# Token tiles 3 and 4 in places that the order sees apart, and A's scores kept negated with a running minimum

## The chip, the cores and the metric

The kernel runs on one core of a Trainium2 chip. A core has a tensor engine (PE in the profile, its weight loads are PEld), a vector engine (DVE), a scalar engine (ACT), a general engine (POOL) and a queue engine (SP) that issues all of this kernel's transfers between the chip's main memory (DRAM) and its on-chip memory. Matrix products land in eight banks of a separate accumulation memory (PSUM). Each engine runs its own instructions strictly in the order in which they were written and waits at an instruction until what it needs has been made by the others. The metric is the device time of one execution in microseconds (us), as the median of several.

## What is computed

One layer of a hybrid encoder over 1024 prompt tokens and 32 sample tokens of width 1024. Cut to what matters here:

```python
hn = rmsnorm(h, g_pre)
qa, ka, va, ga, qb, kb, vb, gb = split(hn @ w_in)           # 8 x 512 columns

# A: band attention, 8 heads of 64
s = einsum('bqhd,bkhd->bhqk', q, k) * ATTN_SCALE
s = s + bias_table[:, clip(k_pos - q_pos, -128, 128) + 128]
s = where(ok, s, -1e30)                                     # own chunk of 64 and 8 before it
oa = softmax(s) @ v

# B: stick-breaking attention, 8 heads of 64 (products of sigmoids along the keys)

y = concat(oa * silu(ga), ob * silu(gb)) @ w_out
h = h + rmsnorm(y, g_post)
h = h + sigmoid(h @ w_ple_gate) * (p @ w_ple)               # "PLE"
```

The keys and values of A and B are outputs too. Everything is float32; a product is made from a high and a low part of each factor (`...h` and `...l`), in three matrix products.

## The kernel before

**The order is made by the program.** The kernel's code does not emit instructions, it records them (`Recorder.add`, line 308). For each argument the recorder keeps a buffer and a *box*: the range of rows and columns that the view covers. An operation comes after every earlier one whose box in the same buffer overlaps its own, if one of the two writes (lines 318 to 330). A view keeps its box exact through slices; `rearrange` (line 76) keeps the box it had and marks all its dimensions unknown, so a slice taken after a `rearrange` still has the box of the whole. `order` (line 372) then plays the engines against modelled costs (`cost`, line 338) and takes for each engine, at each time, the ready operation with the lowest key: its class (`cls` for PE, `low` for the others), then its place in the recording. A transfer that comes after another transfer is ready only when the model has that one landed (lines 417 to 420 and 432). A buffer from a ring (a `tag` with `bufs` places) may be taken when all uses of the buffer that held the place before are done (lines 202 and 374 to 376). What comes out is the written order of each engine; on the chip the waits follow the real addresses.

**The start of the kernel** (lines 1334 to 1400). Nine token tiles of 128 rows (the ninth has the 32 sample tokens) are loaded (`load_x`, line 565), normed and scaled (`scale_x`, line 579: a square with its sum on ACT, two tiny POOL instructions for `rs`, two DVE instructions of 512 columns that multiply by `rs` and by the row `gpre`), transposed on PE four squares at a time (`turn_x`, line 588: a PSUM bank `ptx`, a copy on ACT to `hnh`, a difference on DVE to `hnl`), and so become the right-hand side of the input projection. That is worked off in three chunks of 352 tokens; the first needs tiles 0, 1 and a part of 2, the second goes to the middle of tile 5. For the first column groups kA, qA and vA of the projection (`mm_kA`, `mm_qA`, `mm_vA`) the chunks stand one behind the other. Their weights (`wr_...`) are split into parts by POOL. PE also does a piece of the PLE product for tiles 0 to 3 here (`ple`, six matmuls of 512 columns for each of two halves of a tile, `pieces`, line 1157).

Tiles 0, 1, 2 and 5 to 8 take places in a ring of 3076 columns (`om` in the profile). Tiles 3 and 4 lie in one buffer `x34` (`x` in the profile), in the room that later holds `wTh`.

The PSUM banks: two "mm" for the projection, three "S", two "T" for transposes, one "PV". All `ptx` are from "T". Two of the "S" banks hold the two halves of `gpre` until the last tile is scaled; the third takes the early PLE product of tile 2, first half. Its second half takes the place of the first `gpre`.

**Attention** (`attention`, line 778) runs through eight pairs of heads, A and B in turn, while PE fills up with the projection of the next pair. For a block of 128 queries of A: two matmuls per piece of scores into an "S" bank; on DVE one instruction that adds the bias and takes the maximum along the way (lines 843 to 846; two, the second going on from the first's maximum, where the scores have two pieces; the profile shows it as `CUSTOM_DVE_ANT_0` with a short accumulator read behind it); on DVE the maximum is negated (line 848, `statA<-statA TENSOR_SCALAR`); on ACT the Exp with that as its bias and with its sum; on DVE the reciprocal; on POOL the product; then transposes (`ptwA`) for the values. There are 64 such blocks, and two groups for the sample tokens (`sample_attention`, line 949). The bias comes from a table of eight rows that `bias_rows` (line 606) builds and stores to DRAM; `begin` loads it for a head, and POOL writes -1e30 into two corners. The queries are scaled by 1/8 when ACT takes them from the accumulator (line 748); the sample tokens' queries (`qsS`) are cut from the same place.

```python
dma(xt[0:n], x_prompt[0, t * P:t * P + n, :] if t < 8 else x_sample[0])     # load_x
...
pt = psum(TURN.get((t, kh), "T"), f"ptx{t}_{kh}")                           # turn_x
...
acc = psum(("S", "PV")[t - 2] if t > 1 and self.early else "mm" if self.early else "S", f"ple{t}_{q}")
```

Of the kernel before, what the change touches and what calls it, by code (L numbers as in the profile page):

```python
# [8 lines left out]
F32 = mybir.dt.float32  # L9
F32R = mybir.dt.float32r  # L10
AF = mybir.ActivationFunctionType
ALU = mybir.AluOpType

P = 128
D = 1024
# [7 lines left out]
HD = 64  # L23
NEG = -1e30
EPS = 1e-6
SCALE = HD ** -0.5
# [429 lines left out]
def stream_step(  # L456
# [7 lines left out]
    nc = rec  # L464
# [47 lines left out]
    at = rec.pool(at_stack, tc, name="at", bufs=1)  # L512
    opnd = [at0, at]
    ring0, ring1 = Arena(rec, at, "om", 3076), Arena(rec, at, "be", 3640)
# [48 lines left out]
    x34 = []  # L563

    def load_x(t):
        n = min(P, T - t * P)
        if t == 3:
            x34.append(at.tile([P, ringh.cols], F32, tag="wTh", name="x34")[:, 0:2 * D].rearrange("p (a c) -> p a c", a=2))
        xt = x34[0][:, t - 3] if t in (3, 4) else ring0.tile([P, D], f"x{t}")
        dma(xt[0:n], x_prompt[0, t * P:t * P + n, :] if t < 8 else x_sample[0])  # L570
        return xt, n

    HALF = [slice(0, 512), slice(512, 1024)]
    TURN = {}

    def norm_tile(t, xt, n, gp):
        return turn_x(t, scale_x(t, xt, n, gp), n)
# [28 lines left out]
    def bias_rows():  # L606

        rb = ring0.tile([8, 257], "rb")
        dma(rb, rel_bias[0])
        R = ring1.tile([8, 768], "R")  # L610
        nc.gpsimd.memset(R, 0.0)
        nc.vector.tensor_scalar(R[:, 256:768], R[:, 256:768], rb[:, 0:1], None, ALU.add)
        nc.vector.tensor_copy(R[:, 0:256], rb[:, 0:256][:, ::-1])
        dma(r_dr, R)

# [96 lines left out]
    def col_steps(j):  # L712

        kind, p = order[j]
        ab, k = kind[1], kind[0]
        n = sidx(ab, p)
        box = {}
        steps = []

        def mms(c, part):  # L720
            if part == 0:
                if c == 0:
                    ensure(j)
                    ensure(j + 1)
                    if k != "g":
                        box["st"] = at2.tile([P, T], F32, tag="stg", name=f"st{kind}{p}", bufs=3)
                box["acc"] = psum("mm", f"mm_{kind}{p}_{c}")[:, 0:CH]
            acc = box["acc"]
            cs = slice(c * CH, (c + 1) * CH)
            if k == "g" and part == 0:  # L730
                box["og"] = at2.tile([P, CH], F32, tag="bias", name=f"og{kind}{p}_{c}", bufs=2)
                dma(box["og"], o_dr[n][:, cs])
            W = loaded[j]
            for x in range(part * 24 // PARTS, (part + 1) * 24 // PARTS):
                q, k8 = x // KD, x % KD
                a = W[k8 // 4][1 if q == 1 else 0]
                b = (hnl if q == 2 else hnh)[c]
                nc.tensor.matmul(acc, a[:, k8 % 4, :], b[:, k8, :], start=(x == 0), stop=(x == 23))
            if part < PARTS - 1:
                return  # L740
            if k == "g":
                sg = at2.tile([P, 512], F32, tag="sg", name=f"sg{kind}{p}_{c}", bufs=3)[:, 0:CH]
                nc.scalar.activation(sg, acc, AF.Sigmoid)
                nc.vector.tensor_tensor(sg, acc, sg, ALU.mult)
                nc.gpsimd.tensor_tensor(sg, sg, box["og"], ALU.mult)
                dma(og_dr[n, :, cs], sg)
            elif k == "q":
                nc.scalar.activation(box["st"][:, cs], acc, AF.Copy, scale=SCALE)
            else:
                nc.scalar.copy(box["st"][:, cs], acc)  # L750

        for c in range(NCH):
            for part in range(PARTS):
                steps.append((3.6 / PARTS, lambda c=c, part=part: mms(c, part), GATE_NEEDS.get((kind, p)) if part == 0 else None))

        def after_q():
            src_of["q", ab, p] = box["st"]
            nc.gpsimd.tensor_scalar(qsS[:, slot(ab, p), :], box["st"][:, SEQ:T], 1.0, 1.0, ALU.mult, ALU.mult)

        def after_k():  # L760
            src_of["k", ab, p] = box["st"]
            nc.gpsimd.tensor_scalar(ksS[:, slot(ab, p), :], box["st"][:, SEQ:T], 1.0, 1.0, ALU.mult, ALU.mult)

        def after_v(tok):
            src_of["v", ab, p] = tok
            dma(vs_dr[ab][:, p * P:(p + 1) * P], tok[0:NS, 8, :])

        if k == "q":
            steps.append((0.0, after_q))
        elif k == "k":  # L770
            steps.append((0.0, after_k))
            steps += keys_out(ab, p, lambda: box["st"], *((ak_p, ak_s) if ab == "A" else (bk_p, bk_s)))
        elif k == "v":
            steps += values_out(ab, p, lambda: box["st"], *((av_p, av_s) if ab == "A" else (bv_p, bv_s)), after_v)
        return steps


    def attention(ab, p, h):
# [3 lines left out]
        box = {}  # L782

        def begin():
            if ab == "A":
                bias = at2.tile([P, 640], F32, tag="bias", name=f"bias{nm}", bufs=2)
                dma(bias, bias_src(2 * p + h, P, 0, 640))
                nc.gpsimd.memset(bias[0:HD, 0:HD], NEG)
                nc.gpsimd.memset(bias[HD:P, 576:640], NEG)
                box["bias"] = bias  # L790

        def lo_block(i):
# [20 lines left out]
        def scores(i):  # L813
            L, kd, kl = Lq[h], KDh[h], KLD[h]
            b0 = lo_block(i)
            n = (i + 1 - b0) * P
            k0 = b0 * P
            cut = [0, n] if n <= 512 else [0, n // 2, n]
            w0, w1 = rooms(i)
            pieces = []  # L820
            for j in range(len(cut) - 1):
                s = psum("S", f"S{nm}_{i}_{j}")[:, 0:cut[j + 1] - cut[j]]
                lhs = L[:, i * P:(i + 1) * P]
                ks = slice(k0 + cut[j], k0 + cut[j + 1])
                nc.tensor.matmul(s, lhs, kd[:, ks], start=True, stop=False)
                nc.tensor.matmul(s, lhs, kl[:, ks], start=False, stop=True)
                pieces.append((cut[j], cut[j + 1], s))
            if ab == "B":
                a, b, s = pieces[-1]
                dg = s[:, b - a - P:b - a]  # L830
                nc.vector.tensor_tensor(dg, dg, maskb, ALU.add)
                nc.gpsimd.memset(w0[:, n:n + 1], 1.0)
                for a, b, s in pieces:
                    nc.scalar.activation(w0[:, a:b], s, AF.Sigmoid, scale=-1.0)
                for a, b, s in pieces:
                    nc.scalar.activation(w1[:, a:b], s, AF.Sigmoid)
                for a, b, s in reversed(pieces):
                    rev = w0[:, a + 1:b + 1][:, ::-1]
                    nc.vector.tensor_tensor_scan(rev, rev, s, 1.0 if b == n else w0[:, b + 1:b + 2], ALU.mult, ALU.bypass)
                nc.gpsimd.tensor_tensor(w1[:, 0:n], w1[:, 0:n], w0[:, 1:n + 1], ALU.mult)  # L840
            else:
                m = small.tile([P, 4], F32, tag="stat", name=f"stat{nm}_{i}", bufs=6)
                for j, (a, b, s) in enumerate(pieces):
                    nc.vector.tensor_tensor_reduce(
                        w0[:, a:b], s, box["bias"][:, n - b:n - a][:, ::-1], 1.0,
                        -3e38 if j == 0 else m[:, j - 1:j], ALU.add, ALU.max, m[:, j:j + 1])
                last = len(pieces) - 1
                nc.vector.tensor_scalar(m[:, 2:3], m[:, last:last + 1], -1.0, None, ALU.mult)
                nc.scalar.activation(w1[:, 0:n], w0[:, 0:n], AF.Exp, bias=m[:, 2:3], accum_out=m[:, 3:4])
                nc.vector.reciprocal(m[:, 3:4], m[:, 3:4])  # L850
                nc.gpsimd.tensor_scalar(w1[:, 0:n], w1[:, 0:n], m[:, 3:4], 1.0, ALU.mult, ALU.mult)
            state[i] = w0, w1
# [96 lines left out]
    def sample_attention(ab, gi):  # L949
# [6 lines left out]
        NK = PAST + NS  # L956
# [38 lines left out]
        def scores():  # L995
# [20 lines left out]
            else:  # L1016
                m = small.tile([P, 4], F32, tag="stat", name="stat" + nm, bufs=6)
                for j, (a0, b0, s) in enumerate(pieces):
                    nc.vector.tensor_tensor_reduce(
                        w0[:, a0:b0], s, bx["bias"][:, NK - b0:NK - a0][:, ::-1], 1.0,  # L1020
                        -3e38 if j == 0 else m[:, 0:1], ALU.add, ALU.max, m[:, j:j + 1])
                nc.vector.tensor_scalar(m[:, 2:3], m[:, 1:2], -1.0, None, ALU.mult)
                nc.scalar.activation(w1[:, 0:NK], w0[:, 0:NK], AF.Exp, bias=m[:, 2:3], accum_out=m[:, 3:4])
                nc.vector.reciprocal(m[:, 3:4], m[:, 3:4])
                nc.gpsimd.tensor_scalar(w1[:, 0:NK], w1[:, 0:NK], m[:, 3:4], 1.0, ALU.mult, ALU.mult)
            bx["w1"] = w1
# [829 lines left out]
```

## Time and profile before

| | |
|---|---|
| median of 3 runs | 796.58 us (795.9 to 797.61) |
| the profiled execution | 795.36 us, its span 793.6 us |
| tensor engine clock granted | 1.00 |
| busy: PE, PEld, DVE, ACT, POOL | 778.3, 717.3, 589.7, 537.7, 468.4 us |
| moved by the DMA engines | 153.66 MB, 194 GB/s in the mean |

How to read the rows that follow. In a stretch's row stand its bounds and length, then for PE, PEld, DVE, ACT and POOL the busy time and in brackets the number of instructions, then the granted clock, the busy share of the DMA engines and GB/s. A row of a timeline has the start, the busy time, the engine, the operation, out<-in, the shape and the count of instructions merged into it, and in square brackets how long the engine stood idle before it and what ended that. A row of waits has the engine with the tile it worked on, what it waited for, and the us in total, the times and the longest. A row of a group has the count, then the busy time in us and the mean ns of one, then the idle time before. SPq is the queue engine, and its rows show the issue of a transfer, not its landing; a row of issues gives the KB of each and the median us to landing. Matmuls overlap, so PE's pace is read from the starts, not from the durations.

### The profile page before, as it was taken

To read this page: it belongs to the slowest core of one execution; us is meant where nothing else is said; L and a number is where in the kernel's file an instruction comes from. 1 tells how busy PE (TensorE), PEld (TensorE's weight loads), DVE (VectorE), ACT (ScalarE), POOL (GpSimd) and SP (SyncE) were. 2 spreads that over 40 slices of the span, in tenths; PEclk is the share of its full clock that TensorE was granted. 3 is DMA by queue.
4 is the path that set the end of the run, shared out by engine and by line. 5 is a ranking of instruction groups with operands and counts; after the bars stand their busy time and mean duration, and the time that the engine had idled before them with its cause. 6 is when DMAs were issued, how large, how long until landed. Compare 5 with 4: busy or idle time off the path is not lost.

```text
span 793.6 us, 14512 instructions
## 1 busy us (share of the span) xinstructions
PE 778.3 (98%) x4606; PEld 717.3 (90%) x4606; DVE 589.7 (74%) x1170; ACT 537.7 (68%) x1173; POOL 468.4 (59%) x554
## 2 busy tenths in 40 slices
PE   8999999999999999999999999999999999999997
PEld 6899999899989998999998999999998787888786
DVE  7627778787778686877867788767565677988965
ACT  6636786786797677887766778664436976777651
POOL 6615867775777677554635247647462529599523
PEclk9999999999999999999999999999999999999999
DMA  8419866767876859644524646656579865859854
GB/s 293 140 37 293 212 194 203 190 193 231 216 205 202 236 162 253 146 118 132 140 55 130 165 117 172 224 168 192 151 257 292 283 191 175 297 170 341 276 161 133
DMA packets 161087, 153.66 MB, mean 194 GB/s; under 512 B 38562, under 2 KB 127178, under 8 KB 161011
## 3 DMA queue, kind: packets, MB, share of 16 engines
q1 hardware_dynamic: 161010, 152.73, 64.5%
q8 instruction: 37, 0.61, 0.3%
q14 instruction: 40, 0.32, 0.1%
HBM read 94.45 MB, written 49.83 MB: 182 GB/s over the span
## 4 chain that ended last, share of the span: by engine, by line
PE 75%; ACT 4%; DVE 1%; issue 1%; DMA 0%; POOL 0%; DVEq 0%; ACTq 0%
PE mm_gA L450 6%; PE mm_gB L450 5%; PE mm_qB L450 4%; PE mm_vA L450 4%; PE PVB L450 4%; PE mm_kB L450 4%; PE SB L450 3%; PE mm_qA L450 3%; PE mm_kA L450 3%; PE mm_vB L450 3%; PE PVA L450 3%; PE g1P L450 2%; PE o3P L450 2%; PE o1P L450 2%; PE SA L450 2%; PE g0P L450 2%
## 5 line engine op out<-in xcount | busy, mean ns | idle before, releaser
L450 POOL TENSOR_TENSOR be<-be,om 128x1024 f32<-128x1024 f32 (+8 forms) x66 | 80.3, 1222 | 67.9 <-DVE om L450 34.4
L450 DVE TENSOR_TENSOR_SCAN om<-om,SB 128x384 f32<-128x384 f32 (+5 forms) x96 | 92.2, 967 | 14.9 <-ACT be L450 5.4
L450 POOL TENSOR_SCALAR be<-be,statA 128x640 f32<-128x640 f32 (+3 forms) x64 | 44.0, 692 | 53.6 <-DVE statA L450 37.6
L450 ACT ACTIVATE om<-SB 128x384 f32<-128x384 f32 (+5 forms) x96 | 46.6, 497 | 20.1 <-DVE SB L450 15.6
L450 ACT ACTIVATE be<-SB 128x384 f32<-128x384 f32 (+5 forms) x96 | 46.5, 498 | 13.8 <-DVE om L450 7.2
L450 ACT ACTIVATE be<-om,statA 128x640 f32<-128x640 f32 (+3 forms) x64 | 44.6, 697 | 15.8 <-DVE statA L450 11.3
L450 DVE TENSOR_TENSOR wTl<-ptwA,wTh 128x512 fp32r<-128x512 f32 (+2 forms) x80 | 36.2, 480 | 9.2 <-ACT wTh L450 8.9
L450 ACT CAST wTh<-ptwA 128x512 fp32r<-128x512 f32 (+2 forms) x80 | 32.1, 427 | 12.3 <-PE ptwA L450 10.6
L450 DVE TENSOR_TENSOR wTl<-ptwB,wTh 128x512 fp32r<-128x512 f32 (+3 forms) x64 | 33.7, 546 | 4.7 <-ACT wTh L450 4.2
L450 DVE CUSTOM_DVE_ANT_0 om<-SA,biasA 128x320 f32<-128x320 f32 (+2 forms) x64 | 30.9, 483 | 7.0 <-PE SA L450 5.6
L450 DVE TENSOR_TENSOR wTl<-be,wTh 128x640 fp32r<-128x640 f32 (+1 forms) x24 | 30.7, 1281 | 7.1 <-ACT wTh L450 7.0
L450 ACT CAST wTh<-ptwB 128x512 fp32r<-128x512 f32 (+3 forms) x64 | 29.6, 482 | 8.7 <-PE ptwB L450 5.7
L450 PE MATMUL SB<-kdB,LB 128*128 128x384 f32 (+5 forms) x96 | 33.4, 350 | 0.6 <-DVE om L450 0.6
L450 PE MATMUL SB<-klB,LB 128*128 128x384 f32 (+5 forms) x96 | 33.1, 347 | 0.0
L450 PE MATMUL ptwA<-ident,be 128*128 128x128 f32 x200 | 32.1, 273 | 0.5 <-DVE wTl L450 0.5
L450 PE MATMUL SA<-kdA,LA 128*128 128x320 f32 (+2 forms) x96 | 30.2, 323 | 1.5 <-DVE LA L450 0.8
L450 PE MATMUL ptwB<-ident,be 128*128 128x128 f32 x192 | 29.7, 274 | 0.6 <-POOL be L450 0.6
L450 PE MATMUL SA<-klA,LA 128*128 128x320 f32 (+2 forms) x96 | 29.1, 314 | 0.0
L450 POOL TENSOR_TENSOR oB<-oB,oB 128x256 f32<-128x256 f32 x32 | 24.6, 786 | 6.4 <-issue 3.4
L450 DVE TENSOR_TENSOR SB<-SB,maskb 128x128 f32<-128x128 f32 x64 | 17.6, 290 | 12.5 <-PE SB L450 10.0
L450 POOL TENSOR_TENSOR gB<-gB,gB 128x256 f32<-128x256 f32 x32 | 25.5, 819 | 1.8 <-DMA gB<-in_w_ple_gate_dram 1.4
L450 PEld LDWEIGHTS ptwA<-ident,be 128*128 128x128 f32 x200 | 24.2, 140 | 1.9 <-issue 1.0
(712 smaller groups left out, 2691.7 us busy)
## 6 DMA issues: line engine op xcount, KB each, us to landing
oB<-in_w_out_dram SPq DMA_DIRECT2D x16, 256.0 KB, 4.4
sum_dro<-oB SPq DMA_DIRECT2D x16, 256.0 KB, 2.4
gB<-in_w_ple_gate_dram SPq DMA_DIRECT2D x16, 256.0 KB, 3.8
sum_drg<-gB SPq DMA_DIRECT2D x16, 256.0 KB, 3.0
x<-in_x_prompt_dram SPq DMA_DIRECT2D x16, 256.0 KB, 4.6
h_dr<-h SPq DMA_DIRECT2D x8, 512.0 KB, 4.2
ht<-h_dr SPq DMA_DIRECT2D x8, 512.0 KB, 5.3
raw<-sum_drg SPq DMA_DIRECT2D x16, 256.0 KB, 3.3
```

The costliest lines, as they stand in the source:

```text
L450: getattr(getattr(tc.nc, o.what[0]), o.what[1])(*args, **kw)
```

## The change

Two things, and one beside them.

*Places.* `x34` is no longer rearranged into two parts; tile 3 is columns 0 to 1023 of the buffer and tile 4 columns 1024 to 2047, taken by a plain slice. The addresses on the chip stay the same, the boxes of the two are now apart. Beside it, the entry `(2,0):"S"` gives the first transposed half of tile 2 the third "S" bank.

*Signs.* A's queries get the scale -1/8, and the eight rows of biases are negated once (a DVE instruction on 8 x 257). The corners get +1e30. The scores with their biases are then the negated ones; the running maximum that starts from -3e38 becomes a running minimum from 3e38, which is the negated maximum. The Exp takes it as its bias as it stands and multiplies its input by -1. The instruction that negated the maximum is gone, for the prompt's blocks and for the sample's groups.

```diff
     def load_x(t):
         n = min(P, T - t * P)
         if t == 3:
-            x34.append(at.tile([P, ringh.cols], F32, tag="wTh", name="x34")[:, 0:2 * D].rearrange("p (a c) -> p a c", a=2))
-        xt = x34[0][:, t - 3] if t in (3, 4) else ring0.tile([P, D], f"x{t}")
+            x34.append(at.tile([P, ringh.cols], F32, tag="wTh", name="x34"))
+        xt = x34[0][:, (t - 3) * D:(t - 2) * D] if 3 <= t < 5 else ring0.tile([P, D], f"x{t}")
...
-    TURN = {}
+    TURN = {(2,0):"S"}
...
         dma(rb, rel_bias[0])
+        nc.vector.tensor_scalar(rb, rb, -1.0, None, ALU.mult)
...
-                nc.scalar.activation(box["st"][:, cs], acc, AF.Copy, scale=SCALE)
+                nc.scalar.activation(box["st"][:, cs], acc, AF.Copy, scale=SCALE if ab == "B" else -SCALE)
...
-                nc.gpsimd.memset(bias[0:HD, 0:HD], NEG)
-                nc.gpsimd.memset(bias[HD:P, 576:640], NEG)
+                nc.gpsimd.memset(bias[0:HD, 0:HD], -NEG)
+                nc.gpsimd.memset(bias[HD:P, 576:640], -NEG)
...
                     nc.vector.tensor_tensor_reduce(
                         w0[:, a:b], s, box["bias"][:, n - b:n - a][:, ::-1], 1.0,
-                        -3e38 if j == 0 else m[:, j - 1:j], ALU.add, ALU.max, m[:, j:j + 1])
+                        3e38 if j == 0 else m[:, j - 1:j], ALU.add, ALU.min, m[:, j:j + 1])
                 last = len(pieces) - 1
-                nc.vector.tensor_scalar(m[:, 2:3], m[:, last:last + 1], -1.0, None, ALU.mult)
-                nc.scalar.activation(w1[:, 0:n], w0[:, 0:n], AF.Exp, bias=m[:, 2:3], accum_out=m[:, 3:4])
+                nc.scalar.activation(w1[:, 0:n], w0[:, 0:n], AF.Exp, bias=m[:, last:last + 1], scale=-1.0, accum_out=m[:, 3:4])
```

The lines of the sample's groups (1018 to 1023) change in the same way.

More of the change, by code (lines that the diff above doesn't have):

```diff
@@ L1020, in scores @@
                         w0[:, a0:b0], s, bx["bias"][:, NK - b0:NK - a0][:, ::-1], 1.0,
-                        -3e38 if j == 0 else m[:, 0:1], ALU.add, ALU.max, m[:, j:j + 1])
-                nc.vector.tensor_scalar(m[:, 2:3], m[:, 1:2], -1.0, None, ALU.mult)
-                nc.scalar.activation(w1[:, 0:NK], w0[:, 0:NK], AF.Exp, bias=m[:, 2:3], accum_out=m[:, 3:4])
+                        3e38 if j == 0 else m[:, 0:1], ALU.add, ALU.min, m[:, j:j + 1])
+                nc.scalar.activation(w1[:, 0:NK], w0[:, 0:NK], AF.Exp, bias=m[:, 1:2], scale=-1.0, accum_out=m[:, 3:4])
                 nc.vector.reciprocal(m[:, 3:4], m[:, 3:4])
```

## The prediction, made before the changed kernel was run

> **What bounds the kernel now.** I read the page first (engines, share of the span), then the busy time by stretches, then the list of what the tensor engine (PE) waits for, then the timelines of the first 45 us, where most of the change lies.
>
> ```profile
> PE 778.3 (98%) x4606; PEld 717.3 (90%) x4606; DVE 589.7 (74%) x1170; ACT 537.7 (68%) x1173; POOL 468.4 (59%) x554
> ```
> ```profile
> 0.00:10.00 10.00, 8.37 (x39) 7.27 (x40) 6.03 (x8) 4.75 (x7) 2.96 (x12) 1.00 0.70 236
> 10.00:20.00 10.00, 8.96 (x49) 6.72 (x47) 8.72 (x12) 7.37 (x14) 9.33 (x14) 1.00 1.08 351
> 20.00:30.00 10.00, 9.08 (x59) 8.35 (x58) 4.44 (x10) 5.46 (x13) 9.17 (x14) 1.00 0.76 243
> 30.00:40.00 10.00, 9.84 (x69) 9.45 (x68) 9.10 (x16) 7.69 (x16) 3.04 (x7) 1.00 0.11 30
> ...
> 600.00:700.00 100.00, 100.00 (x445) 79.92 (x445) 74.18 (x112) 76.49 (x159) 54.20 (x56) 1.00 0.74 238
> ...
> 780.00:794.00 14.00, 8.52 (x49) 7.27 (x47) 7.69 (x14) 2.58 (x5) 4.65 (x4) 0.96 0.47 161
> ```
> ```profile
> PE mm_kB L450 <- ACT stvA L450: 1.6, 1, 1.6
> PE PVB L450 <- DVE wTl L450: 1.4, 1, 1.4
> PE idle L450 <- DVE newh L450: 1.3, 1, 1.3
> PE ptx L450 <- DVE be L450: 1.3, 2, 0.9
> PE SA L450 <- DVE LA L450: 0.8, 1, 0.8
> PE ptx L450 <- DVE hnl L450: 0.8, 2, 0.6
> PE SA L450 <- DVE statA L450: 0.7, 1, 0.7
> PE SB L450 <- DVE om L450: 0.6, 1, 0.6
> PE ptwB L450 <- POOL be L450: 0.6, 1, 0.6
> PE ptwA L450 <- DVE wTl L450: 0.5, 1, 0.5
> ```
>
> PE is the bound: it stands idle for 793.6 - 778.3 = 15.3 us in all. The change does not alter what PE has to compute, so it can only move those idle pieces. Their places: 10 - 8.37 = 1.63, 1.04, 0.92 and 0.16 us in the first four stretches, 3.75 together, of which 1.3 is the start itself; some 5.1 us behind the last matmul; and what the other waits of the list come to, 1.6 + 1.4 + 0.8 + 0.7 + 0.6 + 0.6 + 0.5 = 6.2 us, nearly all of the rest, inside the attention stages, each seen once. DVE, ACT and POOL each have a quarter of the span or more to spare, so work taken from them counts only where PE waits for it.
>
> The Trainium skill, on its page "Perfetto Trace Analysis", section "Identifying the Most-Contended Engine", calls the busy share of the matmuls a poor measure of what is left and the share of the weight loads a better one. By it 793.6 - 717.3 = 76 us would be open, and a better order might gain several times what I sum up. The trace here disagrees: between 600 and 700 us the loads are at 79.92 while matmuls of 512 columns follow each other every 100 / 445 = 0.225 us, which is the pace of an undisturbed run of them below.
>
> **The change part by part.**
>
> *Tiles 3 and 4 seen apart.* The order's model now lets x4's load follow x3's at once and lets x3's square start without x4.
>
> ```profile
> 3.07 0.91 SPq L450 DMA_DIRECT2D om<-in_x_prompt_dram  x2
> ...
> 10.30 2.39 SPq L450 DMA_DIRECT2D x<-in_x_prompt_dram  x1
> 12.80 2.52 SPq L450 DMA_DIRECT2D masks<-maskb  x4
> 15.43 0.99 SPq L450 DMA_DIRECT2D om<-in_x_prompt_dram  x2
> 16.51 0.38 SPq L450 DMA_DIRECT2D wr_vA<-in_w_in_dram  x1
> 17.75 0.33 SPq L450 DMA_DIRECT2D x<-in_x_prompt_dram  x1
> ```
> ```profile
> 26.23 1.41 DVE L450 SCALAR_TENSOR_TENSOR be<-om,rs,gpre 128x512 f32<-128x512 f32 x2 [3.83 <-POOL rs L450]
> 27.75 1.41 DVE L450 SCALAR_TENSOR_TENSOR be<-x,rs,gpre 128x512 f32<-128x512 f32 x2
> ```
> ```profile
> 28.65 0.63 PE L450 MATMUL ptx<-ident,be 128*128 128x128 f32 x4 [0.86 <-DVE be L450]
> ```
>
> Now x4's load stands eight places behind x3's, and tile 5 (the `om` row at 26.23) is scaled ahead of tile 3 (the `x` row). PE meets tile 3's transposes 0.86 us early, and the 0.16 us lost from 30 to 40 us fall to the same crowding of norms behind each other. With tile 3 scaled first, both should go: **-1.02 us**. What is late next: x4's issue moves ahead of four mask loads, x5, x6 and the first half of vA's weights, at a time when the DMA engines are full (1.08) and x3's issue took 2.39 us. So these land up to 2.4 us later. The mask loads are read only in B's sample attention. POOL splits vA's weights:
>
> ```profile
> wr_vA<-in_w_in_dram SPq DMA_DIRECT2D x2, 256.0 KB, 5.1
> ```
> ```profile
> 23.23 0.62 POOL L450 CAST wTl<-wr_vA 128x512 fp32r<-128x512 f32 x1
> ...
> 27.69 1.27 POOL L450 TENSOR_TENSOR wTl<-wr_vA,wTl 128x512 fp32r<-128x512 f32 x1
> ```
> ```profile
> 33.19 1.54 PE L450 MATMUL mm_vA<-hnh,wTl 128*128 128x352 f32 x8
> ```
>
> They land about 16.51 + 5.1 = 21.6, 1.6 us before POOL takes them, so POOL is late by 0.8 us, and its last piece, ready at 28.96, is not read before 33.19, or 31.0 if PE gets there 2.2 us sooner: nothing, unless that cover goes, then +0.8. The bounds of this part are -1.08 (all idle time from 20 to 40 us) and +0.8.
>
> *Tile 2's first transposes get the third "S" bank.* They no longer wait for a "T" bank. But that bank was used by the first half of the early PLE product of tile 2 (six matmuls), which now must wait, as the second half does already, until the row `gpre` has been read for the last time.
>
> ```profile
> 17.55 1.41 DVE L450 SCALAR_TENSOR_TENSOR be<-om,rs,gpre 128x512 f32<-128x512 f32 x2 [0.16 <-POOL rs L450]
> ...
> 40.16 1.38 DVE L450 SCALAR_TENSOR_TENSOR be<-om,rs,gpre 32x512 f32<-32x512 f32 x2
> ```
> ```profile
> 19.61 1.26 PE L450 MATMUL ptx<-ident,be 128*128 128x128 f32 x8 [0.62 <-DVE hnl L450]
> 20.93 0.89 PE L450 MATMUL mm_kA<-hnh,wh_kA 128*128 128x352 f32 x4
> ...
> 41.88 0.62 PE L450 MATMUL ple<-wph0True,php 128*128 128x512 f32 x2
> ...
> 43.01 0.39 PE L450 MATMUL ple<-wpl1True,php 128*128 128x512 f32 x1
> ```
>
> Tile 2's first half is scaled at 17.55 + 0.70 = 18.25, its transposes could start at about 18.3 instead of 19.61, and the projection, 1.32 us behind them now, at 19.6 instead of 20.93: -1.31. The six matmuls, five starts in 43.01 - 41.88 = 1.13 us, so 0.226 each and 1.36 together, leave a place where PE would otherwise wait and go to one (past 40 us) where PE is full: +1.36. Together **+0.05 us**. Bounds: +1.36 if the transposes come no sooner (POOL's `rs`, DVE or the copies on ACT hold them), -1.3 if tile 2's chain also moves forward by as much again.
>
> *The sign moved.* One DVE instruction leaves each of 64 prompt blocks and 2 sample groups; one on 8 rows comes in.
>
> ```profile
> L450 DVE TENSOR_SCALAR statA<-statA 128x1 f32<-128x1 f32 x64 | 9.5, 149 | 1.2
> ```
> ```profile
> 42.98 0.46 DVE L450 TENSOR_SCALAR be<-be,om 8x512 f32<-8x512 f32 x1
> ...
> 69.02 0.29 DVE L450 CUSTOM_DVE_ANT_0 om<-SA,biasA 128x128 f32<-128x128 f32 x1 [2.08 <-PE SA L450]
> ```
> ```profile
> ACT be L450 <- DVE statA L450: 11.3, 7, 4.6
> ```
>
> The new one costs under 0.46 us (the row of 512 columns) and sits before a bias that is first read at 69.02, 26 us later: nothing, behind that cover (the bias loads take a few us of it); without it, 0.46. The reduction with min and the Exp with scale -1 are taken to last as long as now; no row shows them, and the bounds are those of their present rows, zero either way. DVE gets back 66 x 0.149 = 9.8 us and each Exp starts one instruction sooner, but this lies beside PE's work: only PE's own wait for `statA`, 0.7 us, names that instruction's neighbours. I take **-0.7**. Bounds: PE's waits for DVE after 60 us, 1.4 + 0.8 + 0.7 + 0.6 + 0.5 = -4.0 at best, and at worst the largest single wait (1.6, a projection's bank that ACT empties late) once more in each of A's four stages: +6.4. Those ends are far apart because the whole order is made from modelled costs and shifts when one cost is taken out.
>
> The sum: -1.02 + 0.05 - 0.7 = -1.67 us. The profiled execution took 795.36 us, 1.22 less than the median of 796.58; it gives 793.7 there and **794.9 us** against the median.
>
> **The rivals.**
>
> *More gain:* the new order also loses one of the two longest waits in the attention stages (1.5 on average). For it: each stands once among hundreds of similar places, so it is an accident of the order. Against it: nothing in the change aims at them, and a new order has its own. -1.67 - 1.5: 793.4; with both, 791.9.
>
> *Nothing to be told:* tile 2's transposes come no sooner, so the gap that the six matmuls leave stays open (+1.36 instead of +0.05) and eats the gain; tile 2's scaling waits for `rs` until 17.55, on a POOL that is 93% busy there. -1.02 + 1.36 - 0.7 = -0.4: 796.2. The same time comes out if the separation does not work on the chip and x4 still waits for x3; against that, the two `om` loads at 3.07 go into one buffer and are issued in 0.91 us without a wait.
>
> *Slower:* ACT runs in its written order. If the order, believing the maximum ready one instruction sooner, puts A's Exp ahead of the copies that empty a projection's bank, ACT waits inside the Exp with the copy behind it, and PE stops for the bank. It does so already: ACT has waited for `statA` up to 4.6 us, and PE 1.6 us for the copy to `stvA`. It decides once the wait in front of an Exp is longer than the one spare bank covers. Two such stops in A's four stages: -1.02 + 0.05 + 3.2 = +2.2: 798.8; four would give 802.
>
> **How the numbers follow.** Chances: forecast 0.42 (own range 793.7 to 796.3), more gain 0.17, nothing 0.16, slower 0.25. A measurement of this kernel can tell about 0.2% (1.6 us) from no change, so the line lies at 795.0, and the forecast's share is cut there: 0.22 of it is faster, 0.20 the same. Faster 0.22 + 0.17 = 0.39; the same 0.20 + 0.16 = 0.36; slower 0.25. The range cuts off the gain of both waits below and more than two ACT stops above: 792.2 to 799.6.
>
> **What would show it.** Right: the first mm_kA starts near 19.6; no wait in front of tile 3's transposes; x4's load directly behind x3's; twelve early PLE matmuls, not six, past 40 us; DVE with 1105 instructions and about 580 us; no PE wait for `statA`. Wrong: PE's idle time from 10 to 20 us above 1.04 with mm_kA still at 20.9 (the second rival), or PE's idle time between 60 and 600 us above 6.2 with ACT waiting for `statA` in front of it (the third). If those idle times fall by more than 2 us, it is the first.

## The result, and the profile after

The changed kernel takes 799.88 us (median of 10 runs, 798.8 to 802.2) against 796.62 us for the kernel before on the same chip (10 runs): the ratio is 1.0044 (1.0036 to 1.0052), so it is slower by 0.4%. The forecast was 794.9 us and "faster"; the time also lies just above the range, which ended at 799.6.

The span and the engines' row, from the page of the kernel after:

```profile
span 798.1 us, 14463 instructions
...
PE 781.2 (98%) x4606; PEld 718.0 (90%) x4606; DVE 586.3 (73%) x1105; ACT 541.7 (68%) x1177; POOL 471.1 (59%) x554
```

DVE lost its 66 negations and gained one instruction (1170 to 1105), as intended; its busy time fell by 3.4 us (589.7 to 586.3), not by the 10 foreseen. Two numbers were not foreseen at all. PE is busy 2.9 us longer (781.2 against 778.3) with the same 4606 matmuls. And ACT, of which the change takes nothing and to which it adds nothing, has *four instructions more* (1177 against 1173) and 4.0 us more work.

The start, from PE's and the queue engine's timelines of the kernel after:

```profile
10.29 2.89 SPq L450 DMA_DIRECT2D x<-in_x_prompt_dram  x2
```
```profile
19.05 0.90 PE L450 MATMUL mm_kA<-hnh,wh_kA 128*128 128x352 f32 x4
...
39.75 0.63 PE L450 MATMUL ple<-wph0True,php 128*128 128x512 f32 x2
...
42.27 0.39 PE L450 MATMUL ple<-wpl1True,php 128*128 128x512 f32 x1
```

The loads of tiles 3 and 4 are issued together, the first projection starts at 19.05 (20.93 before, 19.6 foreseen), and the twelve early PLE matmuls stand from 39.75 on, the last at 42.27. What follows is where the gain is lost again. These are the uses of one tile, first of A's scores in attention and then of the output projection, before:

```profile
L450 PE MATMUL SA<-kdA,LA x96: 220/309/497, 65.7 to 473.2; 128*128 128x320 f32 x64, 128*128 128x128 f32 x8, 128*128 128x256 f32 x8, 128*128 128x384 f32 x8
```
```profile
L450 PE MATMUL o0P<-oB,A11o x12: 389/389/396, 618.1 to 620.6; 128*128 128x512 f32 x12
```

and after:

```profile
L450 PE MATMUL SA<-kdA,LA x96: 220/309/500, 64.2 to 466.1; 128*128 128x320 f32 x64, 128*128 128x128 f32 x8, 128*128 128x256 f32 x8, 128*128 128x384 f32 x8
```
```profile
L450 PE MATMUL o0P<-oB,A11o x12: 387/389/397, 622.6 to 625.2; 128*128 128x512 f32 x12
```

Attention starts 1.5 us sooner (64.2 for 65.7), and the output projection behind it 4.5 us later (622.6 for 618.1). So the start won 1.5 us and attention lost 558.4 - 552.4 = 6.0 us; the spans differ by that sum, 4.5. Each is read from one profiled execution. For the start that is rough: in two kernels below with the same instructions up to there (the places alone, and its control) attention starts at 65.7 and at 64.4 us. Attention itself repeats better: it takes 552.4 to 552.5 us with the order of before (the kernel before, and the one with the order held), and 552.6 to 553.0 with that of the places. Two of the stretches in which attention lost, first before, then after:

```profile
100.00:120.00 20.00, 20.00 (x136) 19.44 (x135) 15.38 (x32) 16.92 (x39) 12.31 (x21) 1.00 0.63 185
...
220.00:240.00 20.00, 19.17 (x128) 17.72 (x127) 16.63 (x41) 19.27 (x42) 15.22 (x26) 1.00 0.69 198
```
```profile
100.00:120.00 20.00, 18.18 (x119) 16.79 (x117) 15.02 (x31) 18.68 (x41) 12.48 (x21) 1.00 0.62 178
...
220.00:240.00 20.00, 17.72 (x119) 16.01 (x118) 14.70 (x35) 19.10 (x39) 11.76 (x18) 1.00 0.65 186
```

In the first, PE does 17 matmuls fewer, and ACT is busy 1.76 us longer. The list of PE's waits between 60 and 600 us names ACT in places where it did not before:

```profile
PE PVA L450 <- ACT wTh L450: 1.7, 2, 0.9
...
PE SB L450 <- ACT be L450: 0.7, 1, 0.7
```

What ACT did there is the timeline of ACT around 105 us in the kernel after, and behind it PE's:

```profile
103.86 1.28 ACT L450 ACT_TABLE_LOAD   x1
105.15 0.28 ACT L450 ACTIVATE om<-SB 128x128 f32<-128x128 f32 x1
...
105.82 1.28 ACT L450 ACT_TABLE_LOAD   x1
107.11 0.83 ACT L450 ACTIVATE be<-om,statA 128x640 f32<-128x640 f32 x1
...
107.94 0.56 ACT L450 CAST wTh<-ptwA 128x512 fp32r<-128x512 f32 x1
108.53 1.28 ACT L450 ACT_TABLE_LOAD   x1
109.82 0.28 ACT L450 ACTIVATE be<-SB 128x128 f32<-128x128 f32 x1
```
```profile
108.56 0.85 PE L450 MATMUL PVA<-wTh,v2A 128*128 128x512 f32 x4 [0.95 <-ACT wTh L450]
110.15 0.51 PE L450 MATMUL SB<-kdB,LB 128*128 128x512 f32 x1 [0.74 <-ACT be L450]
```

`om<-SB` and `be<-SB` are B's Sigmoids, `be<-om,statA` is A's Exp. Each time that ACT goes from one of these functions to the other, an ACT_TABLE_LOAD, the load of a function table, of 1.28 us stands in between; copies between them need none. In the new order B's first Sigmoid comes ahead of A's last Exp, so that the table goes to Sigmoid, back to Exp and to Sigmoid again: three loads that begin within 4.7 us. The copy to `wTh` behind that Exp is late by two of them, and PE stands for 0.95 us; `be` is late by the third, and PE stands for 0.74. In the kernel before, A's last Exp (105.97) comes first and there is one load, behind it:

```profile
105.97 0.83 ACT L450 ACTIVATE be<-om,statA 128x640 f32<-128x640 f32 x1
...
109.61 1.28 ACT L450 ACT_TABLE_LOAD   x1
```

The groups of the whole execution, before and after, count them:

```profile
L450 ACT ACT_TABLE_LOAD x12 | 15.4, 1283 | 0.9 <-PEq L1844 0.7
```
```profile
L450 ACT ACT_TABLE_LOAD x16 | 20.5, 1283 | 1.0 <-PEq L1843 0.7
```

Those are the four additional instructions. ACT's timelines place them: two stand here (three loads against one), two between 225 and 237 us (225.45, 227.77, 230.47, 233.27 and 236.78, where the kernel before has 226.33, 229.66 and 233.42). The chain of waits after shows that they are on the path: from 99.13 to 110.11 us it runs on ACT without a break and goes through all three loads of that place.

```profile
99.13 1.05 ACT LB L450
...
103.86 1.28 ACT L450
...
105.82 1.28 ACT L450
...
108.53 1.28 ACT L450
...
109.82 0.29 ACT be L450
```

### The profile page after: what moved, and what is told of

Its sections match the earlier page's. It is cut to its first block, busy times and chain, and to the rows that moved or that the text cites. A ratio compares the mean times of both kernels' runs of the same rounds, so it can differ in the third digit from the quotient of the medians.

```text
span 798.1 us, 14463 instructions
## 1 busy us (share of the span) xinstructions
PE 781.2 (98%) x4606; PEld 718.0 (90%) x4606; DVE 586.3 (73%) x1105; ACT 541.7 (68%) x1177; POOL 471.1 (59%) x554
## 4 chain that ended last, share of the span: by engine, by line
PE 83%; ACT 6%; DMA 4%; DVE 3%; POOL 2%; issue 1%; SPq 1%; ACTq 0%; DVEq 0%; POOLq 0%
PE mm_gA L450 6%; PE mm_gB L450 6%; PE mm_qA L450 5%; PE mm_kA L450 5%; PE mm_vB L450 5%; PE PVB L450 4%; PE mm_kB L450 4%; PE mm_qB L450 4%; PE SB L450 4%; PE mm_vA L450 4%; PE SA L450 3%; PE g1P L450 2%; PE o3P L450 2%; PE o1P L450 2%; PE PVA L450 2%; PE g0P L450 2%
## 5 line engine op out<-in xcount | busy, mean ns | idle before, releaser
L450 POOL TENSOR_TENSOR be<-be,om 128x1024 f32<-128x1024 f32 (+8 forms) x66 | 84.9, 1289 | 65.6 <-DVE om L450 38.1
L450 ACT ACTIVATE be<-om,statA 128x640 f32<-128x640 f32 (+2 forms) x64 | 44.6, 698 | 16.0 <-DVE statA L450 7.7
L450 PE MATMUL ptwA<-ident,be 128*128 128x128 f32 x200 | 33.7, 274 | 1.3 <-DVE wTl L450 1.2
L450 DVE STREAM_TRANSPOSE om<-be 128x640 f32<-128x640 f32 (+1 forms) x24 | 22.2, 926 | 6.2 <-POOL be L450 5.8
```

What stands on the lines that cost most here:

```text
L450: getattr(getattr(tc.nc, o.what[0]), o.what[1])(*args, **kw)
```

## The experiments

The kernel before was timed beside them on the same chip: 796.35 us with the first two sets (halves, instructions or order), 796.21 with the four loads put in and the three grouped kernels, 796.17 with the loads taken out, the control and the places apart.

**Which half of the change loses.** The places alone (`load_x` and `TURN`), and the signs alone (all other lines of the diff).

> Only the places: the plain slices of x34 and the third S bank for tile 2; signs and maximum as before. Theory (the places shorten the start, and the loss is made by the order of the attention, which shifts because the negation's modelled cost is gone): the start stays 1.5 us shorter, so about 795.1 us. Rival A (the loss comes from removing the negation as such, the minimum or the scale of -1): 795.1 too. Rival B (the loss comes from the new start, which sets the attention off at another time against the transfers): about 800.

> Only the signs and the minimum: x34 rearranged as before, no S bank for tile 2. Theory (order): slower by what the attention lost in the changed kernel, some 4.5 to 6 us over before, so 801 to 802.6. Rival A (the instructions as such): the same. Rival B (the new start): no loss, 796 to 796.6.

Measured: the places 794.51 us, ratio 0.9975 (0.9966 to 0.9984); the signs 800.76 us, 1.0057 (1.0043 to 1.0071), just below the 801 to 802.6 expected. The places gain 1.8 us and the signs lose 4.4. The places alone have 12 table loads, the signs alone 16.

**The instructions or the order.** The signs are changed on the chip, but the planner still sees a negation, with its cost, where none is emitted; so the order is that of before without the negations. The eight rows of biases are negated by the instructions that build their table. Once on the kernel before, once with the places.

```diff
-                nc.vector.tensor_scalar(m[:, 2:3], m[:, last:last + 1], -1.0, None, ALU.mult)
-                nc.scalar.activation(w1[:, 0:n], w0[:, 0:n], AF.Exp, bias=m[:, 2:3], accum_out=m[:, 3:4])
+                rec.add("DVE", lambda *a: None, (m[:, 2:3], m[:, last:last + 1]), {})
+                nc.scalar.activation(w1[:, 0:n], w0[:, 0:n], AF.Exp, bias=As(m[:, 2:3], m[:, last:last + 1]), scale=-1.0, accum_out=m[:, 3:4])
```

`As` is a view that the planner takes for the first argument and the chip for the second.

> The start as before, the signs and the minimum as in the change, but the order is made as if the negation were still there: a ghost of it is recorded with its modelled cost and emits nothing, and the table of biases is negated inside the two instructions that build it. Every engine's written order is that of before, less the 66 negations. Theory (order): no loss, the small relief alone: 795.9 to 796.6. Rival A (the instructions as such): some 4.5 to 6 us over before, 801 to 802.6. Rival B (the new start): 796 to 796.6.

> The places, and the signs with the ghost of the negation in the order. Theory (order): the start's gain and the small relief, no loss: 794.4 to 795.1, the fastest of the four. Rival A (the instructions as such): about 800. Rival B (the new start): about 800.

Measured: 795.84 us, 0.9994 (0.9986 to 1.0003), and with the places 794.63, 0.9982 (0.9974 to 0.9991). With the order held, the minimum, the Exp with scale -1 and 66 DVE instructions fewer make no difference that can be told. The loss is made by the new order that the planner lays out once the negation's cost is gone.

**What in that order: the kernel after with the loads taken out.** Three Sigmoids stand alone between two Exps in the order of the kernel after. They become a Copy, and nothing else in the written order of any engine changes; the kernel leaves out the sigmoid of these three blocks.

```diff
+        lone, run = set(), []
+        for o in [o for o in ops if o.eng == "ACT" and isinstance(o.what, tuple) and o.what[1] == "activation" and o.args[2] in (AF.Exp, AF.Sigmoid)]:
+            if run and run[-1].args[2] != o.args[2]:
+                if len(run) == 1 and run[0].args[2] == AF.Sigmoid:
+                    lone.add(id(run[0]))
+                run = []
+            run.append(o)
...
+                if id(o) in lone:
+                    args[2], kw["scale"] = AF.Copy, 0.0
```

> The kernel after with every instruction in its place on every engine, and each Sigmoid that stands alone between two Exps (three of them, on one 128x128 block each) made a Copy times zero, which needs no function table: 10 loads for 16 and nothing else changed. It leaves out the sigmoid of these three blocks, so B's weights there are not the reference's. If the loads by themselves make the loss: 6 x 1.28 us of ScalarE fewer at the places where TensorE stood still, 793.5 to 796 us against 799.9. If the new order makes it and the loads only happen to stand there: 798.5 to 800.5 us.

Measured: 793.02 us, 0.9958 (0.9944 to 0.9972), below what the first theory expected. Its timeline of ACT at the place shown above, the uses of the output projection's tile, and the group of loads:

```profile
104.73 0.28 ACT L459 ACTIVATE om<-SB 128x128 f32<-128x128 f32 x1
105.25 0.48 ACT L459 CAST wTh<-ptwA 128x384 fp32r<-128x384 f32 x1 [0.24 <-PE ptwA L459]
105.76 0.83 ACT L459 ACTIVATE be<-om,statA 128x640 f32<-128x640 f32 x1
...
106.59 0.57 ACT L459 CAST wTh<-ptwA 128x512 fp32r<-128x512 f32 x1
107.17 1.28 ACT L459 ACT_TABLE_LOAD   x1
108.47 0.28 ACT L459 ACTIVATE be<-SB 128x128 f32<-128x128 f32 x1
```
```profile
L459 PE MATMUL o0P<-oB,A11o x12: 387/389/398, 616.8 to 619.4; 128*128 128x512 f32 x12
```
```profile
L459 ACT ACT_TABLE_LOAD x10 | 12.8, 1283 | 0.9 <-PEq L1852 0.7
```

The instructions are the same in the same order; two of the three loads are gone, and ACT waits for PE (0.24) where PE waited for ACT. Attention's scores start at 64.7 us here, so attention takes 616.8 - 64.7 = 552.1 us, as long as before (552.4), and 6.3 less than after (558.4). With six loads, 7.7 us of ACT, taken out of an order that is otherwise the same, all that attention lost comes back. Two things keep this from being exact. The six are two more than the four additional ones: one load is left at each of the two places, where the kernel before has one and three. And followed matmul by matmul, which the same order allows, PE in the kernel after falls behind by 1.3 us between 100 and 120 us and by 3.0 between 220 and 240, where the loads stood; about 2 us more come later, where no load was taken out, the largest piece (0.8, near 322 us) behind a transfer (`be<-swapB`) for which ACT waits 1.65 us in the kernel after and 0.39 here. How much of that follows from the loads is not shown.

**The reverse: loads put into an order that has none there.** In the kernel with the places alone a Sigmoid of one column is emitted ahead of the last Exp of A's head 1 in both passes, and in a control a Copy of one column instead.

```diff
+    BOUNCE = ((0, 1, 7), (1, 1, 7))
...
+                if (p, h, i) in BOUNCE:
+                    def twice(out, x, f, bias, accum_out):
+                        tc.nc.scalar.activation(accum_out, halfp.get(), AF.Sigmoid)
+                        tc.nc.scalar.activation(out, x, f, bias=bias, accum_out=accum_out)
```

> The places alone, each instruction in the place it had, with a Sigmoid of one column put on ScalarE ahead of the last Exp of A's head 1 in both passes, so that the function table is loaded four times more (16 for 12), as in the kernel after. Its output is the reference's. If table loads in front of A's last Exps make the loss, this costs most of what the kernel after lost in attention: 4 x 1.28 us of ScalarE, of which some is hidden, 797.5 to 799.6 us against 794.5 of the places alone. If the loss comes from the new order of the other engines, and ScalarE hides the loads, 794.3 to 795.3 us.

> The control of the kernel with four loads put in (802.7 us): the places alone, with the same two instructions of one column ahead of the same two Exps, as Copy and not as Sigmoid, so that no table is loaded for them (12). If the loads made the 8.2 us: 794.3 to 795.3 us. If an instruction at that place costs by itself: above 796.

Measured: 802.72 us, 1.0071 (1.0059 to 1.0083), and the control 795.15, 0.9988 (0.9979 to 0.9997), where the places alone had 0.9975 (0.9966 to 0.9984). The timeline of ACT in the first, with one of the two places:

```profile
106.54 1.28 ACT L854 ACT_TABLE_LOAD   x1
...
108.10 1.28 ACT L855 ACT_TABLE_LOAD   x1
109.40 0.83 ACT L855 ACTIVATE be<-om,statA 128x640 f32<-128x640 f32 x1
```

These are exactly four loads more, at the two places at which the kernel after has its four. They cost 802.72 - 795.15 = 7.6 us, more than was expected and 1.9 us each: more than the 1.28 that one lasts. The stretches in which they stand show where, first with the loads, then in the control:

```profile
100.00:120.00 20.00, 17.80 (x117) 16.65 (x117) 12.47 (x27) 18.19 (x39) 11.34 (x20) 1.00 0.62 185
220.00:240.00 20.00, 16.56 (x111) 15.13 (x109) 13.85 (x40) 18.57 (x37) 12.46 (x21) 1.00 0.75 228
```
```profile
100.00:120.00 20.00, 20.00 (x135) 19.32 (x134) 15.98 (x31) 17.45 (x41) 11.83 (x22) 1.00 0.56 171
220.00:240.00 20.00, 19.14 (x127) 17.46 (x126) 15.86 (x39) 19.19 (x42) 15.00 (x24) 1.00 0.72 203
```

PE does 18 and 16 matmuls fewer there, as it did 17 and 9 fewer in the kernel after. Matmul by matmul PE falls behind the control by 2.7 us between 110 and 120 us, about what the two loads there last, and by 4.0 us between 230 and 240; of the 8.2 us between the spans of the two profiled executions (801.1 and 792.9) another 1.2 lies in their starts. So the time above 1.28 us a load comes at the second place; how it comes about was not followed further.

**The change with the loads grouped.** One kernel adds a rule to the recorder; another only a price to the planner.

```diff
+        if method == "activation" and args[2] in (AF.Exp, AF.Sigmoid):
+            if self.table and self.table[0] != args[2]:
+                self.held = self.table[1]
+                self.table = None
+            if self.table is None:
+                self.table = (args[2], [])
+            self.table[1].append(o)
+            o.after.update(self.held)
```
```diff
+                if e == "ACT" and isinstance(o.what, tuple) and o.what[1] == "activation" and o.args[2] in (AF.Exp, AF.Sigmoid):
+                    if table != o.args[2]:
+                        t += 1283
+                    table = o.args[2]
```

> The kernel after, whole, with one rule more for the planner: an Exp is ordered behind every Sigmoid of the run of Sigmoids recorded before it, and a Sigmoid behind every Exp of the run before it, so the table changes 8 times for 16. If the table loads made the loss: 16 - 8 = 8 loads fewer, 10.3 us of ScalarE fewer than the kernel after, 793.5 to 796.5 us. If the new order as a whole made it: 798.5 to 801 us. A rule can cost by itself, where B's first Sigmoids wait for A's last Exp: then it lies between.

> The kernel after with no rule, but with 1283 ns charged in the planner's model whenever ScalarE goes from Exp to Sigmoid or back: the planner is free to choose. 8 loads. If the loss is the planner's blindness to the load: 793.5 to 796.5 us; if not, 798.5 to 801 us.

> The places alone (794.5 us) with the rule that keeps Exps and Sigmoids apart: 8 loads for 12. If four loads are worth what the kernel after lost by four more, 790 to 793 us; if the loads left in the kernel before stand where ScalarE has room, 794 to 795 us.

Measured: the rule 793.35 us, 0.9961 (0.9949 to 0.9973), just below its range; the price 797.21, 1.0014 (0.9999 to 1.0028), inside neither range that was expected of it; the rule with the places alone 794.65, 0.9977 (0.9968 to 0.9986), a miss for the theory that each load is worth time. All three have 8 loads. So the number of loads does not give the time by itself: with the four that the places alone lose by the rule nothing is gained that can be told, while the six of the kernel after were worth 6.9 us. But a rule or a price lays the order out anew, so none of these three runs is a measure of loads alone: with the rule on the places PE's wait for ACT's copy to `stvA` is 2.3 us, where the places alone have 1.6. In the kernel with the price PE's waits are of another kind:

```profile
PE PVB L454 <- ACT wTh L454: 2.6, 1, 2.6
PE SB L454 <- ACT be L454: 1.8, 1, 1.8
PE mm_kB L454 <- ACT wh_kB L454: 1.7, 1, 1.7
```

Three long stops behind ACT at other places, each once, and none with a table load in front of it. At the longest, ACT itself has waited 2.65 us for a transfer (`be<-swapB`, up to 322.16 us). The executions of this kernel spread from 795.0 to 800.6 us and the profiled one took 799.55, so these rows show one of its slower ones; why it spreads was not looked into. The version with the rule beats both kernels, by 0.4% the one before.

**The two places apart.** Only the cut of the buffer (the first two lines of the diff), and only the bank (`TURN`).

> Of the places only the cut of the buffer of tiles 3 and 4, so that the order sees them apart; tile 2's transposes stay in their old banks. The forecast gave this edit -1.02 us (bounds -1.08 to +0.8): 795.2 to 795.7 us. If the bank of tile 2 makes the gain of the two (794.5 us): 796 to 796.6.

> Of the places only the bank: the transposes of tile 2's first half go to one of the three score banks; tiles 3 and 4 stay one buffer to the order. The forecast gave this edit +0.05 us (bounds +1.36 to -1.3): 796.1 to 796.7 us. If the bank makes the gain: 794.5 to 795.2.

Measured: 795.39 us, 0.9992 (0.9983 to 1.0001), and 796.23, 0.9998 (0.9989 to 1.0007), each close to the forecast's value. Together they gave 0.9975 (0.9966 to 0.9984), 1.1 us more than the two gains added; three such intervals leave about 1.2 us open, so it is not shown that the two need each other. The timelines suggest a way: the issue of tile 3's load and the first projection, with the cut alone and with the bank alone.

```profile
10.39 2.88 SPq L450 DMA_DIRECT2D x<-in_x_prompt_dram  x2
```
```profile
21.09 0.89 PE L450 MATMUL mm_kA<-hnh,wh_kA 128*128 128x352 f32 x4
```
```profile
11.26 2.42 SPq L450 DMA_DIRECT2D x<-in_x_prompt_dram  x1
```
```profile
20.01 0.89 PE L450 MATMUL mm_kA<-hnh,wh_kA 128*128 128x352 f32 x4
...
34.78 0.66 PE L450 MATMUL ptx<-ident,be 128*128 128x128 f32 x4 [0.49 <-DVE hnl L450]
36.04 0.66 PE L450 MATMUL ptx<-ident,be 128*128 128x128 f32 x4 [0.60 <-DVE hnl L450]
```

Measured from the issue, the projection comes 10.70 us behind it with the cut alone (10.63 before) and 8.75 with the bank alone (8.76 after): the bank alone makes the start earlier. But then PE meets transposes that wait 0.49 and 0.60 us for their banks past 34 us, and gives part of it back. In the kernel after, with tiles 3 and 4 loaded together, these waits are gone and the gain stays. Attention, too, takes 553.4 us with the cut alone and 553.0 with the bank alone, for 552.4 before and 552.6 with both; the order there shifts with each edit, and that was not followed.

## Why the prediction was wrong

*The failed step* is "the sign moved", at -0.7 us. By itself the edit measured 800.76 - 796.35 = +4.4. The minimum and the Exp with scale -1 cost nothing that can be told, as it took them to (795.84 against 796.35 with the order held). The -0.7 itself stood on PE's wait for `statA`, and that wait was not the negation's: it is 0.7 us still in the kernel with the order held, where the 66 negations are gone, and 0.8 in the kernel after. Above all it priced the order wrongly. The prediction saw that "the whole order is made from modelled costs and shifts when one cost is taken out", used that for the bounds (-4.0 to +6.4, which hold the +4.4, by luck, for they are made of other waits) and then took a value near zero, as if a shifted order were neutral. It never asked what the planner's model leaves out. The model (`cost`, line 338) has no table load, and the rows were there: 12 loads of 1283 ns stand in the groups of the kernel before, six of them on its chain of waits. With them the question would have been how many switches the new order makes.

The Trainium skill states the rule that bears on this: its page "ScalarE: Activation LUTs", section "Rules for kernel authors", asks for work to be grouped by table set, all of one set before the switch, and its section "What ACT_TABLE_LOAD costs" gives 1283 ns for a load, which the rows here agree with to the nanosecond. The same section adds some 1380 ns of drain to each switch. The rows here show none: the copy ahead of the load at 108.53 ends at 107.94 + 0.56 = 108.50, the load lasts from 108.53 to 109.81, and the Sigmoid starts at 109.82. As for the rule, the kernel after bears it out (793.35 us with the loads grouped), the places alone do not (794.65 for 794.51).

*The rival "slower"* gave 798.8, with 802 as its end, and a chance of 0.25. Its sign, its engine and its victim were right: PE stops because ACT, in its written order, comes late with copies. Its mechanism was not. It was to be Exps that wait for `statA` ahead of such copies, and ACT's wait for `statA` fell, from 11.3 us in the prediction's row to

```profile
ACT be L450 <- DVE statA L450: 7.7, 5, 4.4
```

The mark that the prediction set for this rival, more than 6.2 us of idle PE between 60 and 600 us "with ACT waiting for `statA` in front of it", was met in its first half only (540 - 530.8 = 9.2 us, and 6.5 before by the same count): the waits of PE quoted above have table loads in front of them.

*Tiles 3 and 4 apart*, -1.02: measured 795.39 - 796.17 = -0.78, with an interval that reaches zero. The mechanism shows in the trace: x4's load stands with x3's, and of PE's wait of 0.86 us ahead of tile 3's transposes 0.2 is left in the kernel after (0.49 with the cut alone).

*Tile 2's bank*, +0.05: measured +0.06, with an interval of 0.7 us to either side, so that the agreement is luck: the start came forward (by 1.9 us, counted from the issue of tile 3's load, where 1.3 was foreseen), the six matmuls moved, as told, and two waits that were not foreseen took 1.1 us. The two terms were summed as if independent, -0.97; together they measured 794.51 - 796.35 = -1.84, ratio 0.9975 (0.9966 to 0.9984). This error of 0.9 us is small against the first and has the other sign; whether the two need each other stays open.

*The negation of eight rows* at nothing: not seen in any time, as foreseen.

## What to carry to other kernels

Where a program lays out the order of a kernel from modelled costs, no removal is local: before pricing the instruction that leaves, list what the model does not know and what the trace shows all the same (here a 1.28 us table load at each change between Exp and Sigmoid), and ask how often the new order will pay it. To tell an instruction's cost from the order's, keep the planner's input as it was and change only what is emitted; two runs of that kind parted the two here. And compare the number of instructions on each engine first: four more on an engine that the change does not touch named the cause.

## What was not expected of the hardware

A table load on ACT, which is busy 68% of the span, costs TensorE about its own length or more where it delays what TensorE reads next: four put in cost 7.6 us (795.15 to 802.72), 1.9 each, and six taken out gave 6.9 (799.88 to 793.02), 1.1 each. In another place one costs nothing that shows: in the kernel before, PE is busy 20.00 of the 20 us from 100 on, with the load at 109.61 among them. And part of a loss stands in TensorE's busy time, with the same 4606 matmuls: with the six loads the span is 798.1 - 792.3 = 5.8 us longer, of which 781.2 - 780.0 = 1.2 is busy time and the rest idle. The other 1.7 of the 2.9 us by which PE is busier than before stay when the loads are gone; what makes them was not looked into.
